# Four old states per read, updates split around the outputs, and a convolution start taken by pairs of weight rows

## The chip, the cores and the metric

The kernel runs as one program on one core of a Trainium2 chip. The metric is the device time of one execution in microseconds (us). The engines are called by the names of the profile: PE multiplies matrices (PEld loads its weights beside it), DVE, ACT and POOL work on elements, SP only issues transfers, and ACT and POOL issue transfers too. Each engine has a queue of its own and works it off in order; semaphores order the engines among each other.

## What is computed

The reference is one step of a decoder trunk of two layers, each followed by an MLP. The change touches the second layer's mixer alone, apart from two lines at the program's start. There are 512 prompt tokens and 8 samples of 4 tokens (544 columns in all, in two halves of 272), 32 heads of 64 channels in 4 groups, and a state of 128 numbers per channel. Shortened:

```python
z, xbc, dtr = split(x @ w_in)                         # 2048, 3072, 32 columns
conv = conv_b + sum(cat[:, w:w + T] * conv_w[w] for w in range(4))    # cat: 3 old rows, then xbc
xs, B, C = split(silu(conv)); dt = softplus(dtr + dt_bias)
# per chunk, group g and head r; a = dt * A, cs = cumsum(a)
y = (C @ B.T) * exp(seg(cs)) * dt @ xs                # inside the chunk
y = y + (C @ h0) * exp(cs)                            # what the old state h0 gives
h = exp(cs[-1]) * h0 + (exp(cs[-1] - cs) * dt * xs).T @ B
y = rmsnorm((y + d_skip * xs) * silu(z)) * norm_g;  mix = y @ w_out
```

For the prompt the old state of the first chunk is zero and four chunks of 128 follow each other; each of the 8 samples has an old state of its own, which is read (`C @ h0`) and updated.

## The kernel before, in words

**Dense products.** All activations lie with channels on partitions. A dense block takes one 1024x128 weight and one half of 272 columns: `dense` issues 24 matmuls (8 slices `k`, and for each three products of high and low parts, hi·hi, hi·lo, lo·hi) into one accumulation tile `psd`. A weight arrives by a transfer `wraw`, ACT casts it to `whi` (L166), DVE takes the rest as `wlo` (L167). Five such pairs can be held at a time.

**Order of the work.** PE's order is written out by hand: before each dense matmul `tick` counts down the lanes, and a lane whose count has run out issues its next piece of other PE work. The counts are the table `W`. The orders of ACT, DVE, POOL and SP are set by a scheduler from the order in the code and from priorities; evacuations and weight casts have high priority.

**The mixer's stage** runs in the profile from about 688 to 1060 us. It begins with five weights held together: that of `dt` and the first four of the convolution. Their first halves are worked on ahead, their second halves one weight after the other: a block of 24 matmuls, evacuation, and then `post()` of that weight. For `dt` the evacuation is `ev_dt` (L1369, L1370) and the post is `dt_rows`: exp (L1375), a chain of small DVE operations for the softplus (L1376 to L1391), scan (L1401), stores of the cumulative sums to DRAM (`d_cs`, and their exponential `d_ecs`, L1404), and the last product (L1419) that completes the tile `rows`. After `W["dt"]` ticks PE transposes `rows` (`rt`, L1425); DVE copies the result to `scols` and `ncs`.

**Convolution.** `ev_conv` evacuates both halves of a block into a tile `ci` (two buffers; ACT L1445, L1448, L1450), with POOL operations for the three old rows (L1443, L1444) and for the rows to be handed out (L1454, L1455). `post` makes `acc` of it (ACT L1458, three DVE operations L1460) and the SiLU (ACT tanh L1463, DVE L1465).

**Scan of a group** (`group`, lane `ssd`). For each of four chunks and the samples: `scores` loads the decays `E` (512 KB out of `d_cs`, two buffers) and, for chunks 1 to 3, `ec` out of `d_ecs` (L1502), both issued from ACT; PE transposes the inputs (`xt`, L1505) and makes `cb`; DVE scales them twice (`z` and `xw`, L1515, two operations); E becomes exp and is multiplied by `cb` (L1527). `state` carries the state on (`ip`, `sp`), `outputs` makes `yp` of z and E (L1566) and adds it (DVE) and `ec` (POOL, L1571).

**Samples** (`samples`, lane `smp`). Two at a time: PE multiplies their old states with C (`it`, L1613, two column groups at partitions 64 and 96), then makes the four update products `sps` (L1620), and DVE applies them to the states `h0n` (L1626, 32 operations per group). After four such steps `it` is scaled into the spare rows of the tile `z4`, whose `outputs(4)` then adds all.

Of the kernel before, what the change touches and what calls it, by code (L numbers as in the profile page):

```python
# [34 lines left out]
W = dict(dec=12, gates=30, gr=8, sc=16, lev=14, v=24, kd=10, out=38, ss=40, end=12, c0=20, u=13, s=16, ml=12, mr=40, dt=238, sg=72, sx=14, sq=26, so=48, l0=12, l1=12, v0=64, v1=55, f0=16, f1=18)  # L35
# [192 lines left out]
def trunk_kernel(ctx, tc, a, stages=("ab", "mlp0", "ssd", "mlp1")):  # L228
# [139 lines left out]
    def xrhs(k, hf):  # L368
        return xh[hf][:, k, :], xl[hf][:, k, :]

# [946 lines left out]
    def ssd_consts(pool):  # L1317
        con = pool.tile([P, SCONSTS.shape[1]], F32, name="scon", bufs=1)
        nc.sync.dma_start(out=con, in_=a["sconsts"])
        prm = pool.tile([P, 24 * 5 + 16 + 16 + 2], F32, name="sprm", bufs=1)  # L1320
        nc.sync.dma_start(out=prm, in_=a["ssd_prm"])
        V.tensor_scalar(prm[:, :136], prm[:, :136], 0.5, None, ALU.mult)
        cv0 = pool.tile([P, 24, NB, 3], F32, name="cv0", bufs=1)
        nc.sync.dma_start(out=cv0, in_=a["conv0"])
        Cm = pool.tile([P, NB * (NS + LS)], F32, name="Cm", bufs=1)
        G.memset(Cm, 0.0)
        return con, prm, cv0, Cm

    def ssd(pool, ypool, dram, right, ahead, consts):
# [12 lines left out]
        ncp = pool.tile([P, 24, 3], F32, name="ncp", bufs=1)  # L1342
        NX = 3 + NP
        NC = NX + 7 * NB
        rows = pool.tile([P, T], F32, tag="E", name="rows", bufs=2)
# [5 lines left out]
        decs = pool.tile([P, 16, NB], F32, name="decs", bufs=1)  # L1351
        d_cs = dram.tile([32, T], F32, name="d_cs")
# [3 lines left out]
        sb = {}  # L1356
# [64 lines left out]
        def dt_cols():  # L1421
# [5 lines left out]
            for o, b, q in ((slice(0, P), slice(0, 4), p1[:, :384].rearrange("p (b c) -> p b c", b=4)),  # L1427
                            (slice(0, NS), slice(4, 5), p2[:NS, None, :96])):
                V.tensor_copy(cols[o, b], q[:, :, 32:])
                V.tensor_scalar(ncs[o, b], q[:, :, :32], -1.0, None, ALU.mult)  # L1430
            V.tensor_copy(csp, p2[:NS, :32])
            for r in (64, 96):
# [3 lines left out]
        def ev_conv(m, out):  # L1436
# [3 lines left out]
            def ev(hf, ps):  # L1440
                if hf == 0:
                    ci = st["ci"] = cpool.tile([P, NC], F32, tag="ci", name="ci", bufs=2)
                    G.memset(ci[:, 0:3], 0.0)  # L1443
                    G.tensor_copy(ci[:, NX:].rearrange("p (b t) -> p b t", t=7)[:, :, 0:3], cv0[:, m])  # L1444
                    S.copy(ci[:, 3:3 + TH], ps)  # L1445
                    return
                ci = st["ci"]
                S.copy(ci[:, 3 + TH:NX], ps[:, :PB])  # L1448
                cis = ci[:, NX:].rearrange("p (b t) -> p b t", t=7)
                S.copy(cis[:, :, 3:7], ps[:, PB:].rearrange("p (b t) -> p b t", t=LS))  # L1450
            def post():
                ci = st["ci"]
                cis = ci[:, NX:].rearrange("p (b t) -> p b t", t=7)
                G.tensor_copy(ncp[:, m], ci[:, NX - 3:NX])  # L1454
                G.tensor_copy(cv0[:, m], cis[:, :, 4:7])  # L1455
# [7 lines left out]
                S.activation(out[:, :NP], acc[:, :NP], AF.Tanh)  # L1463
                S.activation(o4, v4, AF.Tanh)
                V.scalar_tensor_tensor(out[:, :NP], out[:, :NP], 1.0, acc[:, :NP], ALU.add, ALU.mult)  # L1465
                V.scalar_tensor_tensor(o4, o4, 1.0, v4, ALU.add, ALU.mult)
            return ev, post

        Y, sqs, gates, tanh = [None] * 4, {}, {}, [None]
        lanes.setdefault("smp", [])  # L1470

        def group(g, Bf, Cf):
# [15 lines left out]
            def scores(b):  # L1488
# [3 lines left out]
                if b < 4:  # L1492
                    E = tls[b] = pool.tile([P, 8, P], F32, tag="E", name="E", bufs=2)
                else:
                    tls[b] = pool.tile([P, 8, NS], F32, tag="E4", name="E4", bufs=1)
                    E = tls[b][:NS]
# [10 lines left out]
                TE.matmul(c[:n, :n], Bf[:, tk], Cf[:, tk], start=True, stop=True)  # L1507
                if b < 4:
                    z = pool.tile([P, 512], F32, tag="z", name="z", bufs=2)
                else:  # L1510
                    z = pool.tile([P, 512], F32, tag="z4", name="z4", bufs=1)
                    G.memset(z[NS:2 * NS], 0.0)
                xw = pool.tile([P, 512], F32, tag="xw", name="xw", bufs=2)
                for o, k in ((z, 0), (xw, 32)):
                    V.tensor_tensor(o[:n].rearrange("p (h c) -> p h c", h=8), p[:n].rearrange("p (h c) -> p h c", h=8),  # L1515
                                    cols[:n, b, k + 8 * g:k + 8 + 8 * g, None].broadcast_to([n, 8, 64]), ALU.mult)
# [11 lines left out]
                if b == 4:  # L1528
                    G.memset(tls[b][NS:2 * NS], 0.0)
                    G.tensor_copy(tls[b][64:], seye[64:, None, :].broadcast_to([64, 8, NS]))  # L1530
# [25 lines left out]
            def outputs(b):  # L1556
# [13 lines left out]
                if ec is not None:  # L1570
                    G.tensor_tensor(X[:, :, tk], X[:, :, tk], ec, ALU.add)  # L1571
# [23 lines left out]
            launch(samples(g, X, outputs, tls[4][2], Bs, Xs), "smp")  # L1595

        def samples(g, X, outputs, z, Bs, Xs):
# [3 lines left out]
            for q in range(0, NB, 2):  # L1601
                h0 = [pool.tile([P, 512], F32, tag="h0", name="h0", bufs=4) for _ in range(2)]
                for k in range(2):
                    nc.sync.dma_start(out=h0[k], in_=a["h0"][g, q + k])
                hn = pool.tile([P, 2, 512], F32, tag="h0n", name="h0n", bufs=2)
                nc.sync.dma_start(out=hn, in_=a["h0n"][g, q // 2])
# [3 lines left out]
                yield W["sq"]  # L1610

                for k in range(2):
                    TE.matmul(it[64 + NS * k:64 + NS * k + NS], Cm[:, NS * (q + k):NS * (q + k) + NS], h0[k],  # L1613
                              start=q == 0, stop=q == NB - 2)
                for i in range(2):
# [12 lines left out]
            V.tensor_tensor(z[64:].rearrange("p (h c) -> p h c", h=8), it[64:].rearrange("p (h c) -> p h c", h=8),  # L1628
                            ecs[64:, heads, None].broadcast_to([64, 8, 64]), ALU.mult)
            yield W["so"]  # L1630
            outputs(4)
            ready.add(("Y", g))

# [14 lines left out]
        def square(g, j, hf):  # L1648

            if (j, hf) == (0, 0) and g % 2 == 0:  # L1650
                sqs[g] = ypool.tile([P, 4, TH], F32, name=f"sq{g}", bufs=1)
# [62 lines left out]
        for g in range(4):  # L1714
            if g == 3:
                gate(0)
            Y[g] = ypool.tile([P, 4, T], F32, tag="Y", name="Y", bufs=4)
            evs = [ev_conv(4 * g + j, Y[g][:, j]) for j in range(4)]
            if g == 0:
                evs = [(ev_dt, dt_rows)] + evs  # L1720
                wt = ahead or [(ws.next(), None) for _ in range(HEAD)]
                for hf in range(2):
                    for (w, ps), (ev, post) in zip(wt, evs):
                        if hf == 0 and ps is not None:
                            with tc.high_priority():
                                ev(hf, ps[:, :TH])
                        else:
                            dense(w, xrhs, KT, hf, ev)
                        if hf == 1:
                            post()  # L1730
# [17 lines left out]
        yh0 = hpool.tile([P, 4, T], F32R, name="yh0", bufs=1)  # L1748
        nc.sync.dma_start(out=a["p_conv"], in_=ncp)
        nc.sync.dma_start(out=a["s_conv"], in_=cv0)  # L1750
# [4 lines left out]
        return yh0, Y, gate, sums_of, norms, scaled  # L1755

    def ssd_out(yh0, Y, gate, sums_of, norms, scaled, pool, xp, ypool):
# [41 lines left out]
    while n < len(stages):  # L1799
        st = stages[n]  # L1800
        src = spill
        with ExitStack() as stk:
# [42 lines left out]
            elif st == "ssd":  # L1845
                with tc.tile_pool(name="ssdo", bufs=1, reuse_waits="tile") as pool, \
                        tc.tile_pool(name="hlxs", bufs=2, reuse_waits="tile") as hlx:
                    ws.lend(hlx, "ssdo", 2)
                    ssd_out(*out, pool, xp, ypool)
# [38 lines left out]
def layout(i):  # L1888
# [11 lines left out]
    def seg(n):  # L1900
# [39 lines left out]
    o["conv0"] = i["state_ssd_conv"][0].reshape(NB, 3, 24, P).transpose(3, 2, 0, 1)  # L1940
# [7 lines left out]
            p_h=(4, P, 512), s_h=(4, NB // 2, P, 2, 512), p_conv=(P, 24, 3), s_conv=(P, 24, NB, 3))  # L1948


def unlayout(r):
# [10 lines left out]
                p_conv=r["p_conv"].transpose(2, 1, 0).reshape(1, 1, 3, 3072),  # L1962
                s_conv=r["s_conv"].transpose(2, 3, 1, 0).reshape(1, NB, 3, 3072))
# [21 lines left out]
```

## Time and profile before

| | us |
|---|---|
| runs (three) | 1520.34, 1524.74, 1525.97 |
| median of the runs | 1524.74 |
| profiled execution, its own time | 1517.67 |
| its span (first to last instruction) | 1516.0 |
| around the span | 1.67 |
| mean granted PE clock in it | 0.994 |

A time of a row is the start in the span. "Busy" of an engine is the union of its instructions, so overlapping matmuls count once; the duration of one matmul is longer than its distance to the next, since they are pipelined. In brackets stands the time an engine sat idle ahead of an instruction, and what ended it.

### The profile page before, as it was taken

What the parts mean: (1) busy time and instruction counts of PE and PEld (TensorE: products, weight loads), DVE (VectorE), ACT (ScalarE), POOL (GpSimd) and SP (SyncE); (2) the same over time, 40 slices, a digit from 0 to 9 for tenths busy, and PEclk for the clock granted to TensorE, in tenths of its full rate; (3) what the DMA queues carried; (4) which work ended last, traced back from release to release, by engine and by line L of the source; (5) the groups of instructions that cost most, each with busy time, mean ns of one, the idle gap of its engine ahead of it and who ended that gap; (6) DMA issues with size and microseconds to landing.
All of it is one profiled execution on the core that took longest, in us unless ns stands there. A gap on an engine that the chain in (4) does not pass through costs nothing.

```text
span 1516.0 us, 29158 instructions
## 1 busy us (share of the span) xinstructions
PE 1481.1 (98%) x11637; PEld 1428.0 (94%) x11637; DVE 1093.4 (72%) x1999; ACT 792.1 (52%) x1724; POOL 233.4 (15%) x299
## 2 busy tenths in 40 slices
PE   9999999999999999999999999999999999999997
PEld 9999989999999999999888789899999999999996
DVE  4856676786676766678899978776677677676656
ACT  6645456483543443547775676554257344344333
POOL 0511331100000000023444343420020000000000
PEclk9999999999999999999999999999999999999999
DMA  6321325222233232433457766364222232232221
GB/s 230 94 63 57 116 66 155 83 66 91 91 98 95 87 98 70 153 129 116 126 163 222 231 173 232 98 205 147 71 74 70 94 96 89 95 99 89 65 85 59
DMA packets 88368, 172.10 MB, mean 114 GB/s; under 512 B 9240, under 2 KB 43928, under 8 KB 87976
## 3 DMA queue, kind: packets, MB, share of 16 engines
q1 hardware_dynamic: 55256, 140.09, 29.4%
q10 hardware_dynamic: 30192, 19.41, 4.8%
q0 software_dynamic: 2784, 10.75, 1.9%
q8 instruction: 91, 1.49, 0.4%
q14 instruction: 45, 0.37, 0.1%
HBM read 153.48 MB, written 16.73 MB: 112 GB/s over the span
## 4 chain that ended last, share of the span: by engine, by line
PE 86%; DVE 6%; ACT 5%; issue 2%; DMA 1%; POOL 1%; ACTq 0%; DVEq 0%; POOLq 0%
PE psd L362 58%; PE psd L505 17%; PE num L754 1%; PE yp L1566 1%; DVE wlo L167 1%; PE gs L977 1%; ACT whi L166 1%; PE it L1613 1%; ACT xf L441 1%; PE sp L1544 1%; PE sps L1620 1%; PE ip L1541 1%; PE supd L886 0%; DMA d_ecs<-rows 0%; DVE xf L396 0%
## 5 line engine op out<-in xcount | busy, mean ns | idle before, releaser
L362 PE MATMUL psd<-xh,whi 128*128 128x272 f32 x1504 | 446.5, 297 | 3.4 <-ACT ci L1450 3.0
L362 PE MATMUL psd<-xh,wlo 128*128 128x272 f32 x1504 | 442.2, 294 | 0.0
L362 PE MATMUL psd<-xl,whi 128*128 128x272 f32 x1504 | 439.0, 292 | 2.2 <-DVE xl L282 2.2
L362 PE MATMUL psd<-hh,whi 128*128 128x272 f32 x1024 | 296.4, 289 | 3.6 <-DVE xf L396 2.5
L362 PE MATMUL psd<-hh,wlo 128*128 128x272 f32 x1024 | 295.8, 289 | 0.0
L362 PE MATMUL psd<-hlo,whi 128*128 128x272 f32 x1024 | 295.4, 289 | 0.2
L362 PEld LDWEIGHTS psd<-xh,whi 128*128 128x128 f32 x1504 | 284.7, 189 | 11.5 <-issue 5.4
L362 PEld LDWEIGHTS psd<-xl,whi 128*128 128x128 f32 x1504 | 285.0, 189 | 8.5 <-issue 4.2
L362 PEld LDWEIGHTS psd<-xh,wlo 128*128 128x128 f32 x1504 | 284.6, 189 | 4.4 <-issue 3.1
L167 DVE TENSOR_TENSOR wlo<-wraw,whi 128x1024 fp32r<-128x1024 f32 (+2 forms) x173 | 209.3, 1211 | 64.0 <-ACT whi L166 63.1
L166 ACT CAST whi<-wraw 128x1024 fp32r<-128x1024 f32 (+2 forms) x173 | 174.2, 1011 | 139.2 <-PE psd L362 117.0
L362 PEld LDWEIGHTS psd<-hh,whi 128*128 128x128 f32 x1024 | 192.8, 188 | 5.7 <-DVE xf L396 4.3
L362 PEld LDWEIGHTS psd<-hlo,whi 128*128 128x128 f32 x1024 | 192.8, 188 | 0.7 <-DVE hlo L282 0.6
L362 PEld LDWEIGHTS psd<-hh,wlo 128*128 128x128 f32 x1024 | 192.7, 188 | 0.2
L396 DVE TENSOR_TENSOR xf<-xf,psd 128x272 f32<-128x272 f32 x208 | 88.0, 432 | 78.7 <-PE psd L362 77.7
L505 PE MATMUL psd<-xh,whi 128*128 128x272 f32 x416 | 120.2, 289 | 0.9 <-DVE xf L396 0.9
L505 PE MATMUL psd<-xh,wlo 128*128 128x272 f32 x416 | 119.9, 288 | 0.0
L505 PE MATMUL psd<-xl,whi 128*128 128x272 f32 x416 | 119.6, 288 | 0.0
L202 ACT CAST whi<-wsum 128x1024 fp32r<-128x1024 f32 x52 | 54.3, 1043 | 120.2 <-PE psd L505 72.0
L202 ACT CAST whi<-wraw 128x512 fp32r<-128x512 f32 (+1 forms) x52 | 43.2, 835 | 97.1 <-PE psd L362 83.1
L203 DVE TENSOR_TENSOR wlo<-wsum,whi 128x1024 fp32r<-128x1024 f32 x52 | 63.6, 1224 | 23.2 <-ACT whi L202 23.2
L505 PEld LDWEIGHTS psd<-xh,whi 128*128 128x128 f32 x416 | 78.2, 188 | 1.6 <-DVE xf L396 1.4
(469 smaller groups left out, 2820.4 us busy)
## 6 DMA issues: line engine op xcount, KB each, us to landing
wraw<-mlp_w SPq DMA_DIRECT2D x80, 512.0 KB, 3.7
wraw<-ssd_in SPq DMA_DIRECT2D x40, 512.0 KB, 4.0
wraw<-mlp_w SPq DMA_DIRECT2D x64, 256.0 KB, 3.0
wraw<-ab_in SPq DMA_DIRECT2D x24, 512.0 KB, 3.7
h<-h SPq DMA_DIRECT2D x32, 256.0 KB, 4.1
h0n<-h0n SPq DMA_DIRECT2D x16, 512.0 KB, 4.8
E<-d_cs ACTq DMA_DIRECT2D x16, 512.0 KB, 5.3
s_h<-h0n POOLq DMA_DIRECT2D x16, 512.0 KB, 5.0
```

The source lines that it names most:

```text
L166: nc.scalar.copy(hi[:, r], w[:, r])
L167: nc.vector.tensor_tensor(lo[:, r], w[:, r], hi[:, r].bitcast(F32), ALU.subtract)
L202: self.cut[0] = nc.scalar.copy(hi, x).ins
L203: self.cut[1] = nc.vector.tensor_tensor(lo, x, hi.bitcast(F32), ALU.subtract).ins
L362: last[0] = TE.matmul(ps[:, :TH], wt[:, k, :], rt, start=i == 0, stop=i == n - 1).ins
L396: V.tensor_tensor(x, x, ps, ALU.add)
L441: S.activation(x[:, j], x[:, j], AF.Identity, scale=g[:, j:j + 1], bias=b[:, j:j + 1])
L505: last[0] = TE.matmul(ps, wt[:, k], bt[:, k], start=first and n == 0, stop=n == 11, skip_group_check=not first).ins
L754: TE.matmul(num[i], sT[:, i] if j == i else sT[:, (4, 7, 9)[j] + i - j - 1], vt[key][:, j, h, :w], start=j == 0, stop=j == i)
L977: TE.matmul(p[:, 2 * m * b:2 * m * (b + 1)].rearrange("p (e t) -> p e t", e=2), z[:, 2 * m * b:2 * m * b + P], zq[:, :, m * b:m * (b + 1)] ...
L1541: TE.matmul(ip[:, j * P:(j + 1) * P], hT[:, j * P:(j + 1) * P], Cf[:, tk], start=True, stop=True)
L1544: TE.matmul(sp, Bt[:, b], xw, start=True, stop=True)
```

## The change

It does the following, with the lines of the changed kernel in brackets.

- Old states: `reads(q)` multiplies four samples at once, at four column groups (`it`, L1646), so 8 blocks of four where there were 16 blocks of two. The scaled result is a tile `zs` of its own, and `outputs(4, zs)` issues 8 further matmuls per group (L1603).
- Updates: `writes(q, gap)` holds the four `sps` products and the 8 DVE operations; those of samples 4 to 7 come behind `outputs(4)`. `h0n` is loaded one step ahead; its store moves from POOL's queue to SP's.
- First weights: `by_k` takes the second halves of the five first weights by pairs of slices `k`, 6 matmuls of each weight in turn, so that all five end together; the five `post()` follow.
- Convolution inputs: six places `ci` (three of them in the space of `Y3`) where there were two; POOL's four operations per block are gone, two ACT copies (L1480, L1487) stand for them; tanh is one operation (L1499). The outputs for prompt and samples are one tensor `conv`.
- Scan: three buffers for E, and `z` and `xw` by one DVE operation of 1024 columns per chunk (L1546); `ec` is added on DVE (L1608).
- Start: the second weight is loaded and cast in two parts; the load of `lnp` is issued behind those of x.

```diff
-W = dict(... sq=26, so=48, ...)
+W = dict(... sq=26, st=42, so=10, ...)
...
+            ws._emit([lambda: None] * 2)
             ws.ahead(HEAD)
...
-        nc.sync.dma_start(out=lnp, in_=a["lnp"])
+        with tc.issue_after(loaded):
+            nc.sync.dma_start(out=lnp, in_=a["lnp"])
...
+    def by_k(wts, hf, evacs):
+        ps = [psd.tile([P, 512], F32, tag="d", name="psd") if i < 3 else pm("psd") for i in range(len(wts))]
+        for k0 in range(0, KT, 2):
+            for (hi, lo), p, evac in zip(wts, ps, evacs):
+                for k in (k0, k0 + 1):
+                    rh, rl = xrhs(k, hf)
+                    for i, (wt, rt) in enumerate(((hi, rh), (hi, rl), (lo, rh))):
+                        tick()
+                        last[0] = TE.matmul(p[:, :TH], wt[:, k, :], rt, start=k + i == 0, stop=k == KT - 1 and i == 2).ins
+                if k0 == KT - 2:
+                    with tc.high_priority():
+                        evac(hf, p[:, :TH])
...
-                    E = tls[b] = pool.tile([P, 8, P], F32, tag="E", name="E", bufs=2)
+                    E = tls[b] = pool.tile([P, 8, P], F32, tag="E", name="E", bufs=3)
...
+                    V.tensor_tensor(zx[:, b % 2:b % 2 + 2].rearrange("p k (h c) -> p k h c", h=8),
+                                    p.rearrange("p (h c) -> p h c", h=8)[:, None].broadcast_to([P, 2, 8, 64]),
+                                    dts.broadcast_to([P, 2, 8, 64]), ALU.mult)
...
-                        TE.matmul(ypv[64 * e:64 * e + 64, j], z[:, 64 * r:64 * r + 64], E[:, r], start=True, stop=True)
+                        TE.matmul(ypv[64 * e:64 * e + 64, j], z[:, 64 * r:64 * r + 64], E[:, r], start=True, stop=zs is None)
+                        if zs is not None:
+                            TE.matmul(ypv[64 * e:64 * e + 64, j], zs[:, 64 * r:64 * r + 64], seye, start=False, stop=True)
...
-                    G.tensor_tensor(X[:, :, tk], X[:, :, tk], ec, ALU.add)
+                    V.tensor_tensor(X[:, :, tk], X[:, :, tk], ec, ALU.add)
...
+            def reads(q):
+                h0 = [pool.tile([P, 512], F32, tag="h0", name="h0", bufs=4) for _ in range(4)]
+                for k in range(4):
+                    nc.sync.dma_start(out=h0[k], in_=a["h0"][g, q + k])
+                yield W["sq"]
+                for k in range(4):
+                    TE.matmul(it[NS * k:NS * k + NS], Cm[:, NS * (q + k):NS * (q + k) + NS], h0[k], start=q == 0, stop=q > 0)
...
-                nc.gpsimd.dma_start(out=a["s_h"][g, q // 2], in_=hn)
+                nc.sync.dma_start(out=a["s_h"][g, q // 2], in_=hn)
+            load(0)
+            yield from reads(0)
+            load(2)
+            yield from writes(0, "sq")
+            yield from reads(4)
+            load(4)
...
+            yield from writes(2, "sq")
             yield W["so"]
-            outputs(4)
+            outputs(4, zs)
             ready.add(("Y", g))
+            load(6)
+            yield from writes(4, "st")
+            yield from writes(6, "st")
...
-                        if hf == 1:
-                            post()
+                by_k([w for w, _ in wt], 1, [ev for ev, _ in evs])
+                for ev, post in evs:
+                    post()
```

**Where instructions moved.** First, ACT's queue at the end of the five first weights, before: the second `dtq` evacuation (x2: both quarters) stands behind one cast, and the exp of `dtq` behind one more cast and one convolution's evacuation.

```order
L166 CAST whi<-wraw 128x1024
L1370 ACTIVATE dtq<-psd,sprm 32x136 x2
L166 CAST whi<-wraw 128x1024
L1448 COPY ci<-psd 128x240
L1450 COPY ci<-psd 128x8x4
L1375 ACTIVATE dtq<-dtq 128x136
L1458 ACTIVATE acc<-ci,sprm 128x568
```

The same place now (the exp is L1405; `Y_8232` is one of the places for convolution inputs in the space of `Y3`):

```order
L1483 COPY Y_8232<-psd 128x240
L1485 COPY Y_8232<-psd 128x8x4
L1487 COPY cv_3074<-psd 128x27
L1493 ACTIVATE acc<-Y_8232,sprm 128x568
L1400 ACTIVATE dtq<-psd,sprm 32x136
L1483 COPY ci_8233<-psd 128x240
L1485 COPY ci_8233<-psd 128x8x4
L1487 COPY cv_3074<-psd 128x27
L1493 ACTIVATE acc<-Y_8232,sprm 128x568
L166 CAST whi<-wraw 128x1024
L1405 ACTIVATE dtq<-dtq 128x136
```

The second evacuation of `dt` (L1400) and its exp moved behind convolution work: counted from the end of `dt`'s last matmul, four casts, four convolution evacuations of three copies each and two `acc` stand ahead of the exp now; three of the casts and two of the evacuations are further up than these rows.

Second, DVE's queue at the place where `rows` is complete, before (L1429 and L1430 take the transposed `rt` apart):

```order
L1419 TENSOR_TENSOR rows<-rows 32x544
L1460 SCALAR_TENSOR_TENSOR acc<-ci,sprm,acc 128x568 x3
L167 TENSOR_TENSOR wlo<-wraw,whi 128x1024
L1460 SCALAR_TENSOR_TENSOR acc<-ci,sprm,acc 128x568
L1465 SCALAR_TENSOR_TENSOR Cf<-Cf,acc 128x512
L1466 SCALAR_TENSOR_TENSOR Cf<-Cf,acc 128x32
L1460 SCALAR_TENSOR_TENSOR acc<-ci,sprm,acc 128x568
L1429 COPY scols<-rt 128x256
L1430 TENSOR_SCALAR ncs<-rt 128x128
```

and now (L1449 is what L1419 was):

```order
L1495 SCALAR_TENSOR_TENSOR acc<-ci_8234,sprm,acc 128x568
L1449 TENSOR_TENSOR rows<-rows 32x544
L1500 SCALAR_TENSOR_TENSOR Y_8230<-ci_8234,acc 128x512
L1501 SCALAR_TENSOR_TENSOR Y_8230<-ci_8234,acc 128x32
L1459 COPY scols<-rt 128x2x64
L1462 COPY scols<-rt 128x2x32 x2
L1463 TENSOR_SCALAR ncs<-rt 128x128
```

ACT's queue there, now (L1499 is the tanh, whose result L1500 reads):

```order
L1448 ACTIVATE rows<-rows 32x544
L1537 DMA ec<-d_ecs 64x4x128
L1480 COPY ci_8233<-cv_3074 128x8x3
L1537 DMA ec<-d_ecs 64x4x128 x2
L1499 ACTIVATE ci_8234<-acc 128x568
```

Less other work stands between the completion of `rows` and the use of `rt` than before. A tanh stands behind the issue of `ec`, and the DVE operation that reads it ahead of `scols` and `ncs`; before it was the tanh of `Cf` (L1463), read by L1465.

Third, PE at the samples of group 0, before:

```order
L362 MATMUL psd<-xh_73,whi 128x272
L1613 MATMUL it<-h_9418,Cm 32x512
L1613 MATMUL it<-h_9419,Cm 32x512
L1620 MATMUL sps<-Bm,Xs 128x256 x4
L362 MATMUL psd<-xl_75,whi 128x272
```

and now:

```order
L364 MATMUL psd<-xh_73,whi 128x272
L1646 MATMUL it<-h_9372,Cm 32x512
L1646 MATMUL it<-h_9373,Cm 32x512
L1646 MATMUL it<-h_9374,Cm 32x512
L1646 MATMUL it<-h_9375,Cm 32x512
L364 MATMUL psd<-xl_75,whi 128x272
```

Four old states stand together now, and the `sps` products follow at a place of their own, between other dense matmuls. (In the trace each `it` and `yp` row is two records, so the block of before shows as four matmuls.)

## Rows read from the trace of the kernel before

**Rows 1.** The page: busy time and share of the span by engine.
```profile
PE 1481.1 (98%) x11637; PEld 1428.0 (94%) x11637; DVE 1093.4 (72%) x1999; ACT 792.1 (52%) x1724; POOL 233.4 (15%) x299
```

**Rows 2.** Stretches of the stage: length, busy PE, PEld, DVE, ACT, POOL, clock, DMA.
```profile
705.00:738.00 33.00, 30.54 (x231) 30.32 (x231) 27.59 (x51) 20.62 (x46) 17.02 (x29) 0.95 0.50 137
776.00:850.00 74.00, 72.16 (x560) 60.76 (x560) 69.97 (x124) 51.54 (x154) 31.79 (x51) 1.00 0.68 206
```

**Rows 3.** PE's waits from 688 to 1060, two of them: total, times, longest.
```profile
PE yp L1566 <- DVE ec L1542: 0.7, 1, 0.7
PE sp L1544 <- DVE xw L1515: 0.5, 1, 0.5
```

**Rows 4.** Timeline of PE, 730.8 to 737.5: start, duration, instruction, idle before.
```profile
730.88 0.28 PE L362 MATMUL psd<-xh,wlo 128*128 128x272 f32 x1
733.63 0.40 PE L362 MATMUL psd<-xh,whi 128*128 128x272 f32 x1 [2.46 <-ACT ci L1450]
...
737.39 0.29 PE L362 MATMUL psd<-xh,wlo 128*128 128x272 f32 x1
```

**Rows 5.** Timeline of ACT, 732 to 734.
```profile
732.35 0.66 ACTq L1502 DMA_DIRECT2D ec<-d_ecs  x1
733.13 0.36 ACT L1448 COPY ci<-psd 128x240 f32<-128x240 f32 x1 [4.00 <-DMA d_ecs<-rows]
```

**Rows 6.** Timeline of PE around one block of old states.
```profile
783.00 0.29 PE L362 MATMUL psd<-xh,whi 128*128 128x272 f32 x1
783.22 1.05 PE L1613 MATMUL it<-h,Cm 128*32 128x512 f32 x4
784.20 0.74 PE L1620 MATMUL sps<-Bm,Xs 96*128 96x256 f32 x4
784.78 0.29 PE L362 MATMUL psd<-xl,whi 128*128 128x272 f32 x1
```

**Rows 7.** Timeline of PE in the first layer: 32 matmuls on four column groups.
```profile
158.77 1.08 PE L855 MATMUL snum<-c,Zq 128*32 128x128 f32 x32
```

**Rows 8.** Groups of instructions by form, 688 to 1060: busy, mean ns, idle before.
```profile
L1566 PE MATMUL yp<-E,z 128*64 128x32 f32 x64 | 2.6, 225 | 0.0
L1515 DVE TENSOR_TENSOR z<-xt,scols 128x512 f32<-128x512 f32 x16 | 10.9, 680 | 1.5 <-PE xt L1505 1.5
L1569 DVE TENSOR_TENSOR Y<-Y,yp 128x512 f32<-128x512 f32 x16 | 10.8, 676 | 0.1
```

**Rows 9.** Timelines of ACT, DVE and PE along the dt chain.
```profile
688.24 1.73 ACT L281 CAST xh<-xf 128x544 fp32r<-128x544 f32 x3
...
696.39 0.33 ACT L1375 ACTIVATE dtq<-dtq 128x136 f32<-128x136 f32 x1
696.61 0.86 ACT L1458 ACTIVATE acc<-ci,sprm 128x568 f32<-128x568 f32 x1
...
701.01 1.05 ACT L166 CAST whi<-wraw 128x1024 fp32r<-128x1024 f32 x1 [0.71 <-PE psd L362]
702.04 0.36 ACT L1448 COPY ci<-psd 128x240 f32<-128x240 f32 x1
...
697.34 0.23 DVE L1376 TENSOR_SCALAR dtq<-dtq 128x136 f32<-128x136 f32 x1
...
726.64 0.72 DVE L1419 TENSOR_TENSOR rows<-rows 32x544 f32<-32x544 f32 x1
...
689.69 0.39 PE L362 MATMUL psd<-xl,whi 128*128 128x272 f32 x1 [0.37 <-DVE xl L282]
...
738.02 0.49 PE L1425 MATMUL rt<-scon,rows 96*128 96x96 f32 x4
```

**Rows 10.** Timeline of PE at the start of group 2.
```profile
853.46 1.09 PE L1505 MATMUL xt<-scon,Y 128*128 128x128 f32 x4 [2.39 <-DVE h0n L1626]
854.84 0.77 PE L1507 MATMUL cb<-Cf,Bf 128*128 128x128 f32 x2 [0.29 <-DVE h0n L1626]
```

**Rows 11.** Line L1527 (E times cb): min/median/max ns of one.
```profile
L1527 DVE TENSOR_TENSOR E<-E,cb x20: 405/1225/2302, 743.9 to 975.3; 128x1024 f32<-128x1024 f32 x16, 32x256 f32<-32x256 f32 x4
```

More of the change, by code (lines that the diff above doesn't have):

```diff
@@ L1351, in ssd @@
         decs = pool.tile([P, 16, NB], F32, name="decs", bufs=1)
+        E4 = pool.tile([P, 8, NS], F32, name="E4", bufs=1)
+        z4 = pool.tile([P, 512], F32, name="z4", bufs=1)
+        zx = pool.tile([P, 3, 512], F32, name="zx", bufs=1)
+        G.memset(E4, 0.0)
+        G.memset(z4, 0.0)
+        sq0 = ypool.tile([P, 4, TH], F32, name="sq0", bufs=1)
+        Y = [ypool.tile([P, 4, T], F32, name=f"Y{g}", bufs=1) for g in range(3)] + [None]
+        first = ypool.tile([P, 4, T], F32, tag="Y3", name="Y3", bufs=1).rearrange("p j t -> p (j t)")
+        cis = [first[:, i * (NC + 3):(i + 1) * (NC + 3)] for i in range(3)]
+        cis += [cpool.tile([P, NC + 3], F32, name=f"ci{i}", bufs=1) for i in range(3)]
+        for ci in cis:
+            G.memset(ci[:, 0:3], 0.0)
         d_cs = dram.tile([32, T], F32, name="d_cs")
@@ L1428, in dt_cols @@
                             (slice(0, NS), slice(4, 5), p2[:NS, None, :96])):
[L1429 removed]
+                V.tensor_copy(cols[o, b][:, ::2], q[:, ::2, 32:])
+                if b.stop == 4:
+                    for c in range(2):
+                        V.tensor_copy(cols[o, 1:4:2, 32 * c:32 * c + 32], q[:, 1::2, 64 - 32 * c:96 - 32 * c])
                 V.tensor_scalar(ncs[o, b], q[:, :, :32], -1.0, None, ALU.mult)
             V.tensor_copy(csp, p2[:NS, :32])
[L1432 removed]
+            for r in range(0, P, NS):
                 S.activation(ecs[r:r + NS], ncs[:NS, 4], AF.Exp, scale=-1.0)
@@ L1462, in post @@
                 o4 = out[:, NP:].rearrange("p (b t) -> p b t", t=LS)
[L1463 to L1466, printed above, removed]
+                t4 = ci[:, 3 + NX:].rearrange("p (b t) -> p b t", t=7)[:, :, :LS]
+                S.activation(ci[:, 3:NC], acc[:, :n], AF.Tanh)
+                V.scalar_tensor_tensor(out[:, :NP], ci[:, 3:NX], 1.0, acc[:, :NP], ALU.add, ALU.mult)
+                V.scalar_tensor_tensor(o4, t4, 1.0, v4, ALU.add, ALU.mult)
             return ev, post
-        Y, sqs, gates, tanh = [None] * 4, {}, {}, [None]
+        sqs, gates, tanh, sq_tiles = {}, {}, [None], [sq0]
         lanes.setdefault("smp", [])
@@ L1554, in state, with outputs @@
                     nc.sync.dma_start(out=a["p_h"][g], in_=hn)
-            def outputs(b):
+            def outputs(b, zs=None):
                 E, ec, z, xw = tls.pop(b)
@@ L1594, in group, with samples, load, writes @@
             S.copy(Cm.rearrange("p (q r) -> p q r", r=NS + LS)[:, :, :LS], Cf[:, NP:].rearrange("p (q l) -> p q l", l=LS))
-            launch(samples(g, X, outputs, tls[4][2], Bs, Xs), "smp")
-        def samples(g, X, outputs, z, Bs, Xs):
+            launch(samples(g, outputs, Bs, Xs), "smp")
+        def samples(g, outputs, Bs, Xs):
             heads = slice(8 * g, 8 * g + 8)
             it = psm.tile([P, 512], F32, tag="k", name="it", bufs=1)
-            for q in range(0, NB, 2):
-                h0 = [pool.tile([P, 512], F32, tag="h0", name="h0", bufs=4) for _ in range(2)]
-                for k in range(2):
+            def reads(q):
+                h0 = [pool.tile([P, 512], F32, tag="h0", name="h0", bufs=4) for _ in range(4)]
+                for k in range(4):
                     nc.sync.dma_start(out=h0[k], in_=a["h0"][g, q + k])
-                hn = pool.tile([P, 2, 512], F32, tag="h0n", name="h0n", bufs=2)
-                nc.sync.dma_start(out=hn, in_=a["h0n"][g, q // 2])
+                yield W["sq"]
+                for k in range(4):
+                    TE.matmul(it[NS * k:NS * k + NS], Cm[:, NS * (q + k):NS * (q + k) + NS], h0[k], start=q == 0, stop=q > 0)
+            old = {}
+            def load(q):
+                old[q] = pool.tile([P, 2, 512], F32, tag="h0n", name="h0n", bufs=2)
+                nc.sync.dma_start(out=old[q], in_=a["h0n"][g, q // 2])
+            def writes(q, gap):
+                hn = old.pop(q)
                 Bm = pool.tile([96, 2, P], F32R, tag="Bm", name="Bm", bufs=2)
@@ L1609, in samples @@
                     S.activation(Bm[:, k], Bs.bitcast(F32), AF.Identity, scale=seqm[:96, q + k:q + k + 1])
[L1610 to L1614, printed above, removed]
+                yield W[gap]
                 for i in range(2):
@@ L1721, in ssd @@
                 wt = ahead or [(ws.next(), None) for _ in range(HEAD)]
[L1722 to L1728, printed above, removed]
-                        if hf == 1:
-                            post()
+                for (w, ps), (ev, post) in zip(wt, evs):
+                    if ps is not None:
+                        with tc.high_priority():
+                            ev(0, ps[:, :TH])
+                    else:
+                        dense(w, xrhs, KT, 0, ev)
+                by_k([w for w, _ in wt], 1, [ev for ev, _ in evs])
+                for ev, post in evs:
+                    post()
                 launch(dt_cols(), "dt")
```

77 lines of the change are left out of this document (38 added, 39 removed).

## The prediction

> **What bounds the kernel now.** Read the busy shares first: PE is busy for 98% of the span, DVE for 72% [rows 1]. So the change pays where it takes work or waits from PE, and costs where it makes PE wait. All of it but two lines lies in the mixer's stage, so I read that by stretches: DVE is busy 69.97 of 74.00 us from 776 to 850, beside a PE that is busy for 72.16 [rows 2]. There DVE is nearly as full as PE, though the page's mean hides it; what comes late on DVE has no slack to catch up in. Next, what PE waits for. The longest wait is 2.46 us at 733.63 on a convolution input `ci` [rows 4]. The row names ACT, but ACT itself had stood for 4.00 us, because the issue of `ec` at the head of its queue waited for `d_ecs` to land [rows 5]. After the wait the clock is at its lower level: from 733.63 to 737.39 lie 17 distances that take 3.76 us, where 17 at 0.125 take 2.13, so 1.6 us more. This place costs 2.46 + 1.6 = 4.1 us. Smaller waits: 0.7 on `ec`, 0.5 on `xw` [rows 3], and 2.39 + 0.29 = 2.7 us at the start of group 2, on the state updates `h0n` [rows 10].
>
> **The change, part by part.**
>
> *Old states.* From the last dense matmul to `it` are 0.22 us (0.125 between dense ones, so 0.095 extra), from `it` to `sps` 0.98, from `sps` to the next dense matmul 0.58 [rows 6]: 1.655 us per block, 16 blocks, 26.5 us. Now 8 reads stand alone: 0.095 + 0.98 + about 0.1 to get back (the 0.58 of four `sps` holds such a 0.1 beside four distances of 0.12), 9.4 us; and 16 `sps` blocks stand alone, 0.095 + about 0.48, 9.1 us. That saves 7.9 us if four column groups run in the time of two. The first layer says they do: 32 matmuls of 128 columns on four groups take 1.08 us [rows 7], and one after the other, at half of the 0.125 of 272 columns, they would take 1.9. If they did not, nothing would be saved.
>
> *Rows of the old states in the output.* 8 more `yp` matmuls per group, as many as are there: the 64 records of that shape are busy for 2.6 us in all [rows 8]. Lower bound half of it, upper bound 64 records at half of 0.125, 4.0; I take 2.0, near the row itself, since records of one column group follow each other.
>
> *Waits taken away.* Six `ci` places end the wait of 733.63 at its root (4.1 us); three E buffers and the merged scaling should take the 0.7 and the 0.5. Together 5.3.
>
> *`by_k`, start.* PE's second halves begin at 689.69 [rows 9], and the evacuations of the halves worked ahead stand behind three casts of `xh` (1.73 us from 688.24). Bounds 0 to 1.7; I take 0.8, the middle.
>
> *`by_k`, end.* This is the term that decides. Five weights with 24 matmuls of 0.125 end at 689.69 + 15.1 = 704.7 in either kernel. Before, `dt` came first and was complete at 692.7; now its last matmul is 4 x 6 x 0.125 = 3.0 us ahead of the common end, at 701.7, 9 us later. Then ACT has four casts (1.05 each), four evacuations (0.36 + two of about 0.2) and two `acc` (0.86) ahead of the exp: 4.2 + 3.0 + 1.7 = 8.9, with `dt`'s own evacuation 9.3. So exp starts at about 711.0, where it started at 696.39 [rows 9]: 14.6 us later. From the first DVE operation behind exp (697.34) to the end of the last one (726.64 + 0.72) DVE works without a gap for 30.0 us, mostly on convolutions; its queue now holds much the same mixture between these two (5 `wlo` for 6, 19 `acc` products for 16), so `rows` is complete near 742. PE comes to `rt` at 738.02 in the trace; without the stall of 4.1 and with the 0.8 at the start, at 734.7. It waits about 7.3 us. Dense work cannot fill in: PE's order is fixed, and `rt` stands at the same place. Behind `rt` DVE reads a tanh that ACT has queued behind the issue of `ec`, as before, and only then takes `rt` apart. Before, `rt` was late enough; now the 4.00 of rows 5 lies open. Bounds 0.2 to 5; I take 4. A further 0.6 for the first products, which need the two tiles made next, and 1.6 for the lower clock, as measured after a shorter wait. Sum 13.5, bounds 8 to 17.
>
> *Updates behind the outputs.* `Y` of a group is ready earlier, but the updates of samples 4 to 7 now run into the next group's start, on a DVE queue in which that group's `Bf` and `Cf` and transposes' readers stand too. Group 2 shows the price, 2.7; group 1, which has none now, gets it too. Bounds 0 and 8 (both groups, and longer).
>
> *DVE's load.* The sum with `ec` comes to DVE: 12 at 0.676, 8.1 us. One scaling of 1024 instead of two of 512 (0.676 to 0.680 each) costs about 1.23, the time of E times `cb` [rows 11], 16 times 0.13 less, 2.0. Six more on an engine without slack; I let half of it reach PE, 3.0, bounds 0 and 6.
>
> *Without cost:* ACT's 48 copies of about 0.2 (ACT is busy for 51.54 of 74 us [rows 2]), the stores on SP (weights are a block ahead; without that cover, one late weight costs its landing time), the changes at the start and the single output tensor.
>
> The sum: -7.9 + 2.0 - 5.3 + 0.8 + 13.5 + 2.7 + 3.0 = **+8.8 us**. Against the profiled execution, 1517.67, that is 1526.5; that run lies 7 us under the median of 1524.74, so I add the difference to the median: **1533.5 us**. Its own range is 1529 to 1540.
>
> **A rule against my reading.** E times `cb` takes 1225 ns in the median and up to 2302 [rows 11], so something stretches DVE here and there. The Trainium skill (SBUF — State Buffer, Who interferes with whom) says that DVE operations with two SBUF inputs and GpSimd operations hold one port pair in turn, and the loser blocks for the whole instruction. By that rule DVE would give back what POOL's removed operations took, and my 3.0 would be about 0.
>
> **The rivals.** *Faster:* `dt`'s lateness never reaches PE, because DVE, freed of POOL, works its queue off sooner and ACT's casts come early. Then 13.5 and both DVE terms go, and group 2's wait too: -7.9 + 2.0 - 5.3 + 0.8 - 2.7 = -13.1, 1511.6. For it: the stretched rows above. Against it: it needs `rows` 7 us earlier, and in that stretch DVE has no gap. *Even:* PE's stall comes, but in it DVE and ACT catch up, so the later terms (2.7, 3.0) don't come and group 2's 2.7 goes: +0.4, 1525.1. *Much slower:* the chain ends at its upper bounds (17) and each group then starts late (8, 6): +20.3, 1545; a failure of four column groups, +7.9, would lead to 1541 too. The last weighs little by rows 7.
>
> **How the numbers follow.** About 0.5% (7.6 us) is what a measurement of this kernel can tell from no change. Chances: forecast 0.36, faster rival 0.28, even 0.19, much slower 0.17. A third of the forecast's own range lies within 0.5%, so 0.11 of it goes to "same": faster 0.28, same 0.30, slower 0.42. For eight in ten the range has to hold both signs: it begins just under the faster rival, 1510, and ends at the much slower one, 1546.
>
> **What would show it.** In the changed profile: `it` as 8 blocks of 1 us, `yp` longer by some 2 us; no wait on a `ci` near 731; a wait of PE at `rt` (L1455) of 7 us on DVE and one at `xt` (L1540) behind it; waits of `xt` on `h0n` at groups 1 and 2. The forecast is wrong if `rt` waits under 3 us, if the exp of `dt` (L1405) starts within 5 us of the common end, or if the waits come and something later gives them back.

## The result, and the profile after

The changed kernel takes 1530.39 us (median of 20 runs, 1523.49 to 1534.34); the kernel before takes 1521.26 in the runs taken beside it. The ratio is 1.0059, 95% interval 1.0049 to 1.0069: slower by 9.1 us, where +8.8 was forecast. The two profiled executions differ by more, 1534.34 against 1517.67 us, since the one lies 3.9 over and the other 3.6 under the median of its own kernel; so the traces are good for single waits and blocks, and the medians and ratios for totals.

The page of the changed kernel, busy time by engine:

```profile
PE 1480.3 (97%) x11701; PEld 1433.0 (93%) x11701; DVE 1088.1 (71%) x1998; ACT 794.3 (52%) x1751; POOL 162.9 (11%) x171
```

Against [rows 1] PE is as busy as before within 1 us, although it has more matmuls, and the span is 16.6 us longer: PE waits more. Its single waits over 0.1 us in the mixer's stage (686 to 1080) add up to 26.3 us, where they made 9.7 before. Some of them (total us, times, longest):

```profile
PE rt L1455 <- DVE rows L1449: 8.1, 1, 8.1
PE xt L1540 <- DVE h0n L1671: 3.9, 2, 2.5
PE yp L1601 <- DVE zx L1546: 2.9, 2, 1.9
PE psd L364 <- ACT ci L1479: 2.3, 2, 2.1
PE psd L383 <- ACT Y L1479: 1.5, 1, 1.5
...
PE xt L1540 <- DVE ncs L1463: 0.8, 1, 0.8
```

The first row, a wait that the kernel before does not have, is about half of the 16.6 us. The others together have grown as well, from 9.7 to 18.2 us, and take back much of what the change saves; the experiments show where a part of them comes from. The chain that leads to the first, on ACT (start, duration, idle before):

```profile
702.28 0.36 ACT L1400 ACTIVATE dtq<-psd,sprm 32x136 f32<-32x136 f32 x1
...
706.75 0.37 ACT L1400 ACTIVATE dtq<-psd,sprm 32x136 f32<-32x136 f32 x1
...
709.25 0.33 ACT L1405 ACTIVATE dtq<-dtq 128x136 f32<-128x136 f32 x1
```

then on DVE, and at last on PE:

```profile
711.76 0.22 DVE L1406 TENSOR_SCALAR dtq<-dtq 128x136 f32<-128x136 f32 x1
...
738.16 1.28 DVE L1431 TENSOR_TENSOR_SCAN rows<-rm,rows 32x544 f32<-32x544 f32 x1
...
744.46 0.72 DVE L1449 TENSOR_TENSOR rows<-rows 32x544 f32<-32x544 f32 x1
```

```profile
727.65 0.39 PE L364 MATMUL psd<-xh,whi 128*128 128x272 f32 x1 [2.14 <-ACT ci L1479]
...
745.24 0.90 PE L1455 MATMUL rt<-scon,rows 96*128 96x96 f32 x4 [8.12 <-DVE rows L1449]
...
748.12 1.09 PE L1540 MATMUL xt<-scon,Y 128*128 128x128 f32 x4 [0.75 <-DVE ncs L1463]
```

The exp of `dt` starts at 709.25 where it started at 696.39 [rows 9], and the two parts of its evacuation are 4.5 us apart, with convolution work between. DVE takes 33.4 us from L1406 to the end of L1449, where it took 30.0, and PE reaches `rt` at 737.1 and stands until 745.24. The rows of PE show what else to read: the wait on `ci` is there in a new form, at 727.65.

Old states, on PE:

```profile
793.00 0.29 PE L364 MATMUL psd<-xh,whi 128*128 128x272 f32 x1
793.22 1.07 PE L1646 MATMUL it<-h,Cm 128*32 128x512 f32 x8
794.22 0.39 PE L364 MATMUL psd<-xl,whi 128*128 128x272 f32 x1
794.45 0.29 PE L364 MATMUL psd<-xh,wlo 128*128 128x272 f32 x1
```

Eight records (four matmuls) on four column groups take 1.00 us to the next matmul, where four on two groups took 0.98 [rows 6]; 0.23 instead of 0.125 to the second dense matmul is the way back.

### The profile page after: what moved, and what is told of

Read it like the earlier page. It is cut to its first block, busy times and chain, and to the rows that moved or that the text cites. A ratio compares the mean times of both kernels' runs of the same rounds, so it can differ in the third digit from the quotient of the medians.

```text
span 1532.6 us, 29106 instructions
## 1 busy us (share of the span) xinstructions
PE 1480.3 (97%) x11701; PEld 1433.0 (93%) x11701; DVE 1088.1 (71%) x1998; ACT 794.3 (52%) x1751; POOL 162.9 (11%) x171
## 4 chain that ended last, share of the span: by engine, by line
PE 79%; DVE 9%; ACT 7%; DMA 2%; issue 2%; POOL 0%; ACTq 0%; DVEq 0%; POOLq 0%; SPq 0%
PE psd L364 52%; PE psd L522 17%; ACT whi L166 1%; DVE wlo L167 1%; DVE acc L1495 1%; PE yp L1601 1%; PE num L771 1%; PE psd L383 1%; ACT E L1563 1%; PE gs L994 1%; ACT xf L458 1%; PE sp L1578 1%; DVE h0n L1671 1%; PE ip L1575 1%; DMA s_h<-h0n 0%
## 5 line engine op out<-in xcount | busy, mean ns | idle before, releaser
L364 PE MATMUL psd<-xh,whi 128*128 128x272 f32 x1464 | 436.2, 298 | 2.3 <-ACT ci L1479 2.3
L364 PE MATMUL psd<-xh,wlo 128*128 128x272 f32 x1464 | 431.5, 295 | 0.0
L364 PE MATMUL psd<-xl,whi 128*128 128x272 f32 x1464 | 428.5, 293 | 1.8 <-DVE xl L282 1.8
L364 PEld LDWEIGHTS psd<-xh,whi 128*128 128x128 f32 x1464 | 278.2, 190 | 13.4 <-issue 8.6
L364 PEld LDWEIGHTS psd<-xl,whi 128*128 128x128 f32 x1464 | 278.5, 190 | 10.2 <-issue 6.4
L364 PEld LDWEIGHTS psd<-xh,wlo 128*128 128x128 f32 x1464 | 278.0, 190 | 6.4 <-issue 5.1
L522 PE MATMUL psd<-xh,whi 128*128 128x272 f32 x416 | 120.2, 289 | 0.8 <-DVE xf L413 0.8
L522 PE MATMUL psd<-xh,wlo 128*128 128x272 f32 x416 | 119.7, 288 | 0.0
L522 PE MATMUL psd<-xl,whi 128*128 128x272 f32 x416 | 119.5, 287 | 0.0
L522 PEld LDWEIGHTS psd<-xh,whi 128*128 128x128 f32 x416 | 78.2, 188 | 1.5 <-DVE xf L413 1.3
```

What stands on the lines that cost most here:

```text
L364: last[0] = TE.matmul(ps[:, :TH], wt[:, k, :], rt, start=i == 0, stop=i == n - 1).ins
L522: last[0] = TE.matmul(ps, wt[:, k], bt[:, k], start=first and n == 0, stop=n == 11, skip_group_check=not first).ins
```

## The experiments

All kernels but one start from the changed one. Ratios are to the kernel before, with 95% intervals; two kernels that were not run side by side are compared by their ratios. A trace is one execution, and two of them lie far from their medians: that of the run without by_k 4.3 us over (1523.59), that of the run with `dt` ahead 7.5 us under (1516.43). Single waits can be read from these, differences between totals cannot.

**Without by_k.** The second halves go one weight after the other, each with its post.

```diff
...
-                by_k([w for w, _ in wt], 1, [ev for ev, _ in evs])
-                for ev, post in evs:
-                    post()
+                for hf in range(2):
+                    for (w, ps), (ev, post) in zip(wt, evs):
+                        if hf == 0 and ps is not None:
+                            with tc.high_priority():
+                                ev(0, ps[:, :TH])
+                        else:
+                            dense(w, xrhs, KT, hf, ev)
+                        if hf == 1:
+                            post()
```

> The changed kernel, but the five first weights' second halves one weight after the other again, each followed by its post, as before. If by_k is what makes dt late: the exp of dt starts about 13 us earlier (near 697), PE waits under 1 us at rt instead of 8.1, and the time falls by 8 to 13 us, to 1517 to 1522. Rival, that the wait comes from the other parts (more work on DVE, six convolution places): rt still waits over 5 us and the time stays above 1527. Second rival, that the wait goes but the time is lost again at the group starts: rt waits under 1 us and the time falls by less than 3 us.

1519.3 us, ratio 0.9985 (0.9972 to 0.9997), 11 us less than the changed kernel. No wait at `rt` is left (waits of PE in the stage, the longest; then ACT, DVE and PE along the chain):

```profile
PE yp L1601 <- DVE zx L1546: 2.9, 2, 1.9
PE cb L1542 <- DVE Cf L1500: 2.4, 1, 2.4
PE psd L364 <- ACT Y L1479: 1.8, 1, 1.8
PE xt L1540 <- DVE h0n L1671: 1.8, 2, 1.4
```

```profile
694.67 0.32 ACT L1405 ACTIVATE dtq<-dtq 128x136 f32<-128x136 f32 x1
...
722.74 0.72 DVE L1449 TENSOR_TENSOR rows<-rows 32x544 f32<-32x544 f32 x1
...
735.95 0.49 PE L1455 MATMUL rt<-scon,rows 96*128 96x96 f32 x4
```

The exp starts 14.6 us earlier, `rows` is complete 21.7 us earlier, and PE finds it done. by_k makes the wait; more work on DVE or the six places do not make it alone. The wait on `ci` near 727 is 0.34 us here, so the 2.14 of the changed kernel is by_k's too. The 1.8 us at the stage's start (`Y`, L1479) are there without by_k and are not its price.

**dt ahead of by_k.** One dense block for `dt`, its post, then the four convolutions by pairs.

```diff
-                by_k([w for w, _ in wt], 1, [ev for ev, _ in evs])
-                for ev, post in evs:
+                dense(wt[0][0], xrhs, KT, 1, evs[0][0])
+                evs[0][1]()
+                by_k([w for w, _ in wt[1:]], 1, [ev for ev, _ in evs[1:]])
+                for ev, post in evs[1:]:
                     post()
```

> The changed kernel, but only the four convolution weights go by pairs of slices; dt's second half is one block ahead of them, with its post. If only dt's lateness matters: rt waits under 1 us and the time is within 3 us of that of the run without by_k. Rival, that the four convolutions arriving together fill DVE's queue enough to delay dt's chain alone: rt waits 3 to 7 us and the time lies between the two.

1523.94 us, 1.0016 (1.0001 to 1.0032): between the two, as the rival had it, but not by its wait at `rt`: `rows` is complete at 706.8 and PE doesn't wait there. It waits 3.4 us on `ci`, 3.1 more than without by_k:

```profile
PE psd L364 <- ACT ci L1479: 3.4, 1, 3.4
```

```profile
727.48 0.86 ACT L1493 ACTIVATE acc<-ci,sprm 128x568 f32<-128x568 f32 x1 [0.86 <-DVE Y L1501]
728.25 0.36 ACT L1479 COPY ci<-psd 128x272 f32<-128x272 f32 x1
728.52 0.36 ACT L1483 COPY ci<-psd 128x240 f32<-128x240 f32 x1
```

Four convolutions that arrive together are worked off by DVE one after the other; ACT, whose tanh and `acc` wait for DVE, has the next evacuation behind them, and PE waits for that. The changed kernel has the same wait at 727.65, shorter. Six places for `ci` don't prevent it: here ACT's queue is what is full, not the places. That this wait makes the whole difference to the run without by_k (4.7 us by the ratios) is not shown, since both traces lie far from their medians.

**rt later.** The changed kernel with `dt=300` for 238.

> The changed kernel with one number other: rt comes 62 dense matmuls later (dt=300 for 238), 7.8 us of dense work ahead of it. If the wait at rt is PE time simply lost: rt waits about 0 to 1 us and the time falls by 5 to 8 us. Rival, that the scan as a whole is what is late (each group starts that much later and DVE is the bound): the wait at rt goes, but the waits at the groups' starts and the end of the stage take it back, and the time falls by less than 2 us or grows.

1520.54 us, 0.9993 (0.9980 to 1.0006): 10 us less than the changed kernel, somewhat more than the 5 to 8 expected.

```profile
PE rt L1455 <- DVE rows L1449: 0.9, 1, 0.9
```

With 62 dense matmuls ahead of it PE arrives 0.9 us too early instead of 8.1, and nothing takes it back: the other waits of the stage add up to 18.2 us in both traces. The wait was PE time lost.

**The sum with ec on POOL**, without by_k:

```diff
-                    V.tensor_tensor(X[:, :, tk], X[:, :, tk], ec, ALU.add)
+                    G.tensor_tensor(X[:, :, tk], X[:, :, tk], ec, ALU.add)
```

> As the run without by_k, and the sum with ec back on POOL (12 operations, 8.1 us less on DVE). If DVE's load reaches PE as predicted (3 us for 6): 1 to 4 us faster than the run without by_k. Rival, that POOL's operations slow those of DVE beside them by as much as they take from it: within 1 us of it, or slower, with longer DVE operations beside L1608.

1521.21 us, 1.0002 (0.9986 to 1.0018), not to be told from 0.9985 (0.9972 to 0.9997), and in any case not faster: the rival. What DVE is spared it pays elsewhere. Without these 12 operations (8.2 us) it is busy in the stage for 304.43 us, where it is busy for 302.08 with them (the row of the run without by_k stands further down):

```profile
690.00:1057.00 367.00, 349.77 (x2833) 322.33 (x2833) 304.43 (x533) 234.29 (x639) 94.03 (x82) 0.98 0.56 174
```

One of the operations that pay is E times `cb`; its median stays and its longest grows (min/median/max ns, with the sum on POOL, then with it on DVE):

```profile
L1564 DVE TENSOR_TENSOR E<-E,cb x20: 405/1216/2292, 744.6 to 979.5; 128x1024 f32<-128x1024 f32 x16, 32x256 f32<-32x256 f32 x4
```

```profile
L1564 DVE TENSOR_TENSOR E<-E,cb x20: 406/1215/1414, 743.2 to 981.3; 128x1024 f32<-128x1024 f32 x16, 32x256 f32<-32x256 f32 x4
```

**Stores on POOL's queue**, without by_k (`nc.gpsimd` for `nc.sync` at the store of `hn`):

> As the run without by_k, with the stores of the updated states on POOL's queue again. If the stores on SP are covered as predicted: within 1.5 us of the run without by_k, and the waits at the groups' starts (h0n) as there. Rival, that a store which waits on SP for its h0n holds the transfers queued behind it: 3 us or more faster, with fewer waits on h0n and on DMA.

1517.3 us, 0.9979 (0.9964 to 0.9994). The interval overlaps that of the run without by_k; the stores on SP cost nothing that these runs can show. The waits on `h0n` did not stay as they were: 3.8 us in this trace, 1.8 in that one.

**z and xw apart**, without by_k: two operations of 512 for the one of 1024.

> As the run without by_k, with z and xw by two DVE operations of 512 again instead of one of 1024 (same tiles, z first). If the wait of yp for the scaled tile (2.9 us in two places) comes from the longer operation, it falls by about half and the time by 1 to 2 us; against it stand 16 times 0.14 us more on DVE, 2.2 us. Rival, that DVE's total sets it: 0 to 2 us slower.

1521.13 us, 1.0001 (0.9988 to 1.0015): no gain. The wait of `yp` for the scaled tile did not fall by half either (3.7 us, where it was 2.9), so nothing shows it to come from the longer operation. A loss of about 2 us, the rival, can't be told from none: the intervals overlap.

**Old states by two**, without by_k: a pause of 6 dense matmuls between the second and the third read.

```diff
                 for k in range(4):
+                    if k == 2:
+                        yield 6
                     TE.matmul(it[NS * k:NS * k + NS], ...
```

> As the run without by_k, but four old states are read as two blocks of two with 6 dense matmuls between, so 16 blocks again. If four column groups run in the time of two, the eight extra blocks cost 8 times about 1.2 us: 8 to 10 us slower. Rival, that a block's time goes by its number of matmuls: within 3 us of the run without by_k.

1522.15 us, 1.0014 (1.0002 to 1.0027): 2.9 us more by the medians, 4.4 by the ratios, where 8 to 10 were expected. The blocks do cost what was said:

```profile
779.64 1.05 PE L1648 MATMUL it<-h,Cm 128*32 128x512 f32 x4
780.62 0.39 PE L364 MATMUL psd<-xl,whi 128*128 128x272 f32 x1
...
781.69 1.05 PE L1648 MATMUL it<-h,Cm 128*32 128x512 f32 x4
782.68 0.39 PE L364 MATMUL psd<-xh,wlo 128*128 128x272 f32 x1
```

Half as many matmuls take the same 0.98 us. Summed over the stage, beyond the 0.125 of each dense distance and with the ways in and back, `it` takes 18.9 us against 10.7 in the run without by_k, 8.2 more. But PE's waits in the stage fall from 19.0 to 14.4 us (single waits over 0.1, summed), so about half of what PE saves by reading four at once it spends waiting. How large this share really is stays open, since the trace without by_k lies over its median.

**rt a little later**, without by_k: `dt=252`, then 266 and 245, then 252 with the stores on POOL; and the kernel before with 252.

> As the run without by_k, with rt 14 dense matmuls (1.8 us) later. The wait of xt for ncs (1.66 us) is the only one behind rt there; if it is lost PE time, it falls to about 0 and the time falls by 1 to 2 us. Rival, that DVE then is later for the first group: within 1 us or slower.

1511.13 us, 0.9938 (0.9918 to 0.9957), the fastest kernel of this study: 8 us under the run without by_k by the medians, 7 by the ratios, not 1 to 2. The wait of `xt` on `ncs` (1.66 us) went, but 1.2 us on `Bt`, which ACT makes, stand in its place; the waits on `h0n` at the groups' starts went too (the longest that are left):

```profile
PE cb L1542 <- DVE Cf L1500: 2.1, 1, 2.1
PE psd L364 <- ACT Y L1479: 1.8, 1, 1.8
PE yp L1601 <- DVE zx L1546: 1.7, 2, 1.2
```

All waits of the stage add up to 12.6 us instead of 19.0, and its granted clock is 1.00 where it was 0.98 (stretches from 690 to the end of the stage, of the run without by_k and of this one; length, busy PE, PEld, DVE, ACT, POOL, clock):

```profile
690.00:1059.00 369.00, 350.15 (x2823) 322.22 (x2822) 302.08 (x543) 233.61 (x635) 70.92 (x66) 0.98 0.57 172
```

```profile
690.00:1047.00 357.00, 344.62 (x2826) 318.22 (x2825) 302.22 (x543) 234.31 (x636) 70.58 (x66) 1.00 0.58 178
```

DVE does the same work in both. The two traces are 12 us apart, of which about 4 are the place of the first over its median. Is it slack or a lucky place?

> Without by_k, rt 7 matmuls later (dt=245). If the time follows slack: between the runs at 238 and 252, about 1515. Rival, a matter of place: outside of these two by more than 1.5 us, or as at 238.

1516.08 us, 0.9975 (0.9961 to 0.9989).

> Without by_k, rt 28 matmuls later (dt=266). If it is the slack that a later start gives to DVE: as fast as with 252, within 2 us. Rival, that 252 happens to put the groups' starts between other work: back by 3 us or more towards the run without by_k at 238.

1513.73 us, 0.9968 (0.9957 to 0.9980).

> The kernel before with rt 14 matmuls later (dt=252), nothing else. If the 8 us that this number gave in the changed kernel without by_k come from how its groups then fall against the convolutions: the kernel before, whose groups are built otherwise, changes by less than 3 us. Rival, that the number alone is a better one: 5 to 9 us faster too.

1517.57 us, 0.9988 (0.9979 to 0.9996).

> The run without by_k and with rt 14 matmuls later, and the stores of the updated states on POOL's queue. If the two gains are separate: 1 to 3 us faster than the former, about 1509. Rival, that both took away the same waits at the groups' starts: within 1.5 us of it.

1511.9 us, 0.9959 (0.9947 to 0.9971); not to be told from 252 alone.

245 and 266 lie between 238 and 252, by 1.5 and 2.6 us under 238 by the ratios, but their intervals overlap that of 238; only 252 is clear of it, with either queue for the stores. So whether 7 or 28 matmuls help as well is not settled. What the traces agree on is the wait that goes: on `h0n` PE waits 1.8 to 5.3 us at the starts of groups 1 and 2 in the four runs without by_k that keep 238 and the reads by four, and 0.4, 0, 0 and 1.6 us in those with 245, 252 (twice) and 266. The kernel before gains about 2 us by the number, at most 3, so the rest of the gain hangs on how the changed groups are built. Which of the changed parts it is was not tried.

## Why the prediction was right, and where single terms were not

**The deciding term** stood as put. The exp of `dt` was to start near 711.0 and started at 709.25, `rows` to be complete near 742 and was at 745.2, PE to wait 7.3 us at `rt` and waited 8.12. The runs without by_k and with the later `rt` take 11 and 10 us away. From the start of the stage to the second `xt` (745.40 before, 755.99 now) the trace loses 11.2 us (it enters the stage 0.6 ahead); the terms that fall there (-4.1, -0.5, +0.8, +13.5) make 9.7.

The exp came earlier than put because durations were added up where starts follow closer: ACT goes on 0.41 us after the first of an evacuation's three copies (703.62 to 704.03), where 0.76 was counted. So it starts 4.9 us behind the end of by_k's last matmul:

```profile
704.03 0.29 PE L383 MATMUL psd<-xh,wlo 128*128 128x272 f32 x1
```

By the letter that is a sign of being wrong, "within 5 us of the common end"; the wait, which by that sign should have been missing, was there all the same.

**Inside it, sizes were off.** The wait of `xt` behind `rt` was put at 4 and was 0.75: `d_ecs` had landed when ACT came to it, so ACT did not stand for long at the issue of `ec`, and the 4.00 of [rows 5] did not lie open. DVE's stretch was put at 30.0, as "much the same mixture", and took 33.4: three products of `acc` more for one `wlo` less make 1.0 us by the distances of before (0.72 and 1.14), two more pairs of SiLU operations (L1500, L1501) 1.4, and DVE stood idle 0.9 longer. And the root of the old `ci` wait was not all of it: the 2.46 us went, but 2.14 at 727.65 came, through ACT's queue; I had taken six places to end the wait. The start of by_k was put at 0.8; PE waits 1.5 there, but 1.8 without by_k, so the reason given for that term was not the right one.

**Old states.** Put at -7.9. Counted as the prediction counts, beyond the dense distances and with the way back, the 16 blocks of before took 26.7 us; now the reads take 10.9 and the `sps` blocks 8.7, together -7.1. A read alone costs 1.19 us, as put (1.175); two of the eight, at 807.33 and 868.35, fell where dense matmuls start 0.227 apart, the lower clock, and took 1.76 and 1.97. The rows of old states in the output were put at +2.0 and cost 2.2. Right in kind and nearly in size. What the prediction did not see is that such PE time is no longer all time: by the run with pairs only 3 to 4 of the 8.2 us show.

**DVE's load** is the step that failed: "six more on an engine without slack". DVE's busy time in the stage fell (before, from 690 to 1053; then the changed kernel):

```profile
690.00:1053.00 363.00, 353.58 (x2764) 318.93 (x2763) 306.85 (x546) 231.25 (x611) 141.26 (x195) 0.99 0.57 175
```

```profile
690.00:1070.00 380.00, 354.97 (x2830) 326.07 (x2830) 300.18 (x543) 232.89 (x633) 71.74 (x66) 0.96 0.56 167
```

306.85 to 300.18 us, with POOL at 71.74 instead of 141.26. So it is 6.7 less, not 6 more: operations that stood beside POOL's are short again (E times `cb` has a mean of 1263 ns now and had 1464; the large product of the SiLU and `sq` fell by 3.1 and 1.7 us in all). The rule of the Trainium skill (SBUF — State Buffer, Who interferes with whom), one port pair in turn, was the better guide here, and the run with the sum on POOL agrees with it: its longest E times `cb` is back at 2292, and DVE is no less busy for what POOL took over. The faster rival rested on the same fact; it fell because `dt`'s chain does not wait for POOL but for its place in two queues.

**Group starts** were put at +2.7: `xt` and `cb` wait 2.9 us at group 1 (2.47 on `h0n` and 0.43) and 2.4 at group 2, where it was 2.7. That is as put. It is not the late `dt` that shows there again: without by_k group 1's wait is 0.34 in one trace, but 3.26, 2.34 and 2.26 in three others, where `dt` is early as well (the longer of the two waits in the runs with the sum on POOL, the stores on POOL's queue and the split):

```profile
PE xt L1540 <- DVE h0n L1671: 4.9, 2, 3.3
PE xt L1540 <- DVE h0n L1671: 3.8, 2, 2.3
PE xt L1540 <- DVE h0n L1671: 3.6, 2, 2.3
```

That fits the updates behind the outputs, with a size that small shifts of place decide; no run moved the updates back to show it.

**The total** came out within half a us of the forecast by luck. by_k was put at +14.3 (13.5 and 0.8), and taking it out gives 11.2 by the ratios; all other terms were put at -5.5, and the run without by_k is 2.3 us under the kernel before (0.5 to 4.3). Each half is 3 us off, one way and the other: too much for `xt` and for DVE's load, too little for `rt`, `yp`, `ci` and the waits that take back what `it` saves. The forecast time, 1533.5, is 3.1 over the measured one, since it stood on three runs of the kernel before (1524.74) and twenty have 1521.26. The sum of the much slower rival is +20.6, not +20.3; nothing hangs on that.

## What to carry to other kernels

Work that is finished together arrives together: before several results are made to end at the same time, ask which of them begins the longest chain, and let that one end first. A count that places a step by hand has to be set again when what it waits for moves; 14 matmuls were worth 7 to 8 us here once the cause of the wait was gone. Where two engines are both nearly full, take a saving on one of them at a fraction until a run has shown it.

## What had not been expected of the hardware

Four column groups cost PE the time of two, which the prediction had read from the first layer and these runs show for 512 columns: 8 records in 1.00 us against 4 in 0.98. Not expected was that POOL's operations cost DVE more than had been put for them: POOL gave up 69.5 us in the stage, and DVE's busy time fell by 6.7 although it took over 12 operations of 0.686 us, 8.2 in all (the merged scaling accounts for about 2 of the difference). And the stage's granted clock differs between kernels of the same work, 0.96, 0.98 and 1.00, with the waits. Stretches of three or more dense distances near 0.227 us, the lower of the two clock levels (1.2 of 2.4 GHz), hold 20 distances in the stage of the trace before, 52 in that of the changed kernel, 42 without by_k, and 11 each with `dt=300` and with `dt=252` alone; at 0.1 us each that is 2, 5, 4 and 1 us. After the 8.12 us at `rt` dense matmuls start 0.23 apart from 749.65 to 752.60:

```profile
749.65 0.43 PE L364 MATMUL psd<-xh,wlo 128*128 128x272 f32 x1
749.88 0.43 PE L364 MATMUL psd<-xh,whi 128*128 128x272 f32 x1
...
752.37 0.43 PE L364 MATMUL psd<-xh,wlo 128*128 128x272 f32 x1
752.60 0.43 PE L364 MATMUL psd<-xh,whi 128*128 128x272 f32 x1
```
